# Loading both inputs of a batched matmul through one DMA queue, with the cast moved from the DMA to VectorE

## The chip, the cores and the metric

The kernel runs on one core of a Trainium2 chip. A core has TensorE (PE, matrix products, with its weight loads shown as PEld), VectorE (DVE), ScalarE (ACT), GpSimd (POOL) and SyncE (SP). Data moves between the chip's memory (HBM) and the core's SBUF by 16 DMA engines. Three engines issue transfers: SyncE (its queue is q1 in the profile), ScalarE (q10) and GpSimd (q0; in this kernel some of its transfers also convert fp32 to bf16 on the way). The metric is the device time of one execution in microseconds.

## The reference

```python
def setup_inputs():
    return {
        "a": np.random.randn(1024, 64, 64).astype(np.float32),
        "b": np.random.randn(1024, 64, 64).astype(np.float32),
    }

def reference(a, b):
    return np.matmul(a, b).astype(np.float32)
```

There are 1024 independent products of 64x64 matrices. a and b are read once (16.78 MB each) and the output of 16.78 MB is written once.

## The kernel before

Work is cut into tiles of 64 batches: `n_t` = 16 tiles, t = 0 to 15. a is handled in `n_s` = 8 parts of 128 batches, s = 0 to 7, so part s serves tiles 2s and 2s+1. One part of a is 2 MiB, made of four quarters h of 512 KiB with 4 KB rows (`a_v`); one tile of b is 1 MiB in runs of 512 B (`b_v`); one tile of output is 1 MiB (`o_v`). All operands are turned to bf16 before the products.

What happens to a part of a: `load_a(s)` brings it in. For s = 1 to 7, GpSimd's queue loads three quarters and converts them to bf16 during the transfer (`a_sb`, line 73), and SyncE's queue loads the fourth as fp32 (`a_raw`, line 77). Part 0 is different: `load_first_a` brings all four quarters as fp32, two by SyncE and two by ScalarE, into two tiles of the output pool (line 90). `regroup(s)` then builds `a_bf`, with the four quarters interleaved: for s = 0 four conversions shared by VectorE and ScalarE (line 105), else on VectorE one copy of 3072 bf16 elements per partition (line 108) and one conversion of 1024 (line 111). `transpose(s, j)` turns it on TensorE, pairs of bf16 seen as one fp32 (line 120), and ScalarE copies the result out of PSUM into `at_sb` (line 123).

What happens to a tile t: `spread(t)` makes four VectorE copies into a block-diagonal operand `at_bd` (line 133; two such buffers). `cast(t)` converts the tile of b: on VectorE (line 144), for t = 0 on ScalarE, and for the last tile in four pieces, two on ScalarE and two on VectorE (lines 149 and 151). `multiply(t)` does 64 products of 128x128 by 128x64 (line 189) and copies the results out of PSUM into `o_sb` by eight copies (line 177), on ScalarE, with two of the eight on VectorE where t is odd. `store(t)` sends the tile to HBM (line 166): from GpSimd's queue for t below 14, from SyncE's and ScalarE's for 14 and 15.

`load_b(t)` uses SyncE's queue for even t and ScalarE's for odd t (line 96). `a_pool` and `b_pool` have three buffers for each kind of tile, `o_pool` eight, `work` two. A load waits until the tile that had its buffer before has been used: b(t+3) waits for the cast of b(t).

The order of the work is written out by hand, and each engine carries out its instructions in that order. Before the loop, a part 0, b tiles 0 and 1, a part 1, b tile 2 and a part 2 are loaded, and part 0 is regrouped, transposed and spread. Iteration t then does spread(t+1) and cast(t+1), `load_b(t+3)`, for even t a load of a, transposes, multiply(t), for even t the regroup of part t/2+2, and store(t-1). So, on VectorE, the regroup stands behind the cast of the next tile, and in the last iterations the cast of the last tile stands in front of ScalarE's copies of tile 14. On GpSimd loads of a and stores share one instruction stream; on ScalarE the loads of odd b tiles stand among its copies.

Of the kernel before, what the change touches and what calls it, by code (L numbers as in the profile page):

```python
# [8 lines left out]
fp32 = mybir.dt.float32  # L9
bf16 = mybir.dt.bfloat16  # L10
# [3 lines left out]
def kernel(  # L14
# [14 lines left out]
    nc = tc.nc  # L29
    B, M, K = a.shape  # L30
    _, _, N = b.shape
    assert (M, K, N) == (64, 64, 64) and B % 128 == 0

    n_t, n_s = B // 64, B // 128
    A_AHEAD = 3
# [4 lines left out]
    a_v = a.rearrange("(s g h) (mp v) k -> s h g mp (v k)", h=4, g=32, v=16)  # L40
    b_v = b.rearrange("(t g h) (kp u) n -> t (h kp) g (u n)", h=4, g=16, u=2)
# [3 lines left out]
    a_pool = ctx.enter_context(tc.tile_pool(name="a_pool", bufs=A_AHEAD))  # L45
    b_pool = ctx.enter_context(tc.tile_pool(name="b_pool", bufs=B_AHEAD))
    work = ctx.enter_context(tc.tile_pool(name="work", bufs=2))
    o_pool = ctx.enter_context(tc.tile_pool(name="o_pool", bufs=8))
    t_psum = ctx.enter_context(
        tc.tile_pool(name="t_psum", bufs=4, space=bass.MemoryType.PSUM)  # L50
    )
# [9 lines left out]
    a_tiles, b_tiles, abf_tiles, at_tiles, bbf_tiles = {}, {}, {}, {}, {}  # L61
# [6 lines left out]

    def load_a(s):

        a_sb = a_pool.tile([128, 3, 16, 64], bf16, name="a_sb")
        for h in range(3):
            nc.gpsimd.dma_start(  # L73
                out=a_sb[:, h, :, :].rearrange("p v k -> p (v k)"), in_=a_v[s, h], single_packet=True
            )
        a_raw = a_pool.tile([128, 16, 64], fp32, name="a_raw")
        nc.sync.dma_start(out=a_raw[:].rearrange("p v k -> p (v k)"), in_=a_v[s, 3])  # L77
        a_tiles[s] = a_sb, a_raw

    def load_first_a():  # L80

        raw = [
            o_pool.tile([128, 8, 2, 2, 64], fp32, name="o_sb")[:].rearrange(
                "p gh j wl n -> p (gh j wl n)"
            )
            for _ in range(2)
        ]
        parts = [raw[h % 2][:, 1024 * (h // 2) : 1024 * (h // 2) + 1024] for h in range(4)]
        for h in range(4):
            (nc.scalar if h % 2 else nc.sync).dma_start(out=parts[h], in_=a_v[0, h])  # L90
        a_tiles[0] = parts

    def load_b(t):
        b_sb = b_pool.tile([128, 16, 128], fp32, name="b_sb")
        queue = nc.scalar if t % 2 else nc.sync
        queue.dma_start(out=b_sb[:], in_=b_v[t])  # L96
        b_tiles[t] = b_sb

    def regroup(s):
        a_sb = a_tiles.pop(s)  # L100
        a_bf = work.tile([128, 16, 4, 64], bf16, name="a_bf")
        if s == 0:
            for h in range(4):
                copy = nc.scalar.copy if h % 2 else nc.vector.tensor_copy
                copy(a_bf[:, :, h, :], a_sb[h].rearrange("p (v k) -> p v k", v=16))  # L105
        else:
            cast_sb, raw = a_sb
            nc.vector.tensor_copy(  # L108
                a_bf[:, :, 0:3, :], cast_sb[:].rearrange("p h v k -> p v h k")
            )  # L110
            nc.vector.tensor_copy(a_bf[:, :, 3, :], raw[:])  # L111
        abf_tiles[s] = a_bf
        at_tiles[s] = work.tile([128, 2, 32, 2, 4, 4], fp32, name="at_sb")

    def transpose(s, j):
        a_cols = abf_tiles[s][:].rearrange("p v h k -> p v (h k)").bitcast(fp32)
        for wl in range(2):
            at_ps = t_psum.tile([128, 4, 128], fp32, name="at_ps")
            for vo in range(4):
                nc.tensor.transpose(  # L120
                    at_ps[:, vo, :], a_cols[:, 4 * vo + 2 * j + wl, :], identity[:]
                )
            nc.scalar.copy(  # L123
                at_tiles[s][:, j, :, wl, :, :],
                at_ps[:].rearrange("p vo (g mp) -> p g mp vo", mp=4),
            )

    def spread(t):
        half = slice(16 * (t % 2), 16 * (t % 2) + 16)
        bd = bd_tiles[t % N_BD]  # L130
        for h in range(4):
            rows = slice(32 * h, 32 * h + 32)
            nc.vector.tensor_copy(  # L133
                bd[rows, :, :, :, h, :].rearrange("p j g wl mo -> p j (g wl) mo"),
                at_tiles[t // 2][rows, :, half, :, :, :].rearrange(
                    "p j g wl mp vo -> p j (g wl) (mp vo)"
                ),
            )

    def cast(t):  # L140
        b_bf = work.tile([128, 16, 128], bf16, name="b_bf")
        b_sb = b_tiles.pop(t)
        if t < n_t - 1:
            (nc.vector.tensor_copy if t else nc.scalar.copy)(b_bf[:], b_sb[:])  # L144
        else:
            for gq in range(4):
                rows = slice(4 * gq, 4 * gq + 4)
                if gq % 2:
                    nc.vector.tensor_copy(b_bf[:, rows, :], b_sb[:, rows, :])
                else:  # L150
                    nc.scalar.copy(b_bf[:, rows, :], b_sb[:, rows, :])  # L151
        bbf_tiles[t] = b_bf

    def store(t):
        for piece in held.pop(t):
            piece()
# [51 lines left out]
            held[t] = [lambda q=q: put(q, 8 if whole else 4) for q in ([0] if whole else [0, 4])]  # L208

    with tc.manual_schedule():  # L210
        load_first_a()

        nc.vector.memset(warm[:, 0:1], 0.0)
        nc.scalar.copy(warm[:, 1:2], warm[:, 0:1])  # L214
        load_b(0)
        load_b(1)
        nc.vector.memset(bd_tiles[0][:], 0.0)  # L217
        make_identity(nc, identity)
        nc.gpsimd.memset(bd_tiles[1][:, 0], 0.0)
        load_a(1)  # L220
        load_b(2)
        nc.gpsimd.memset(bd_tiles[1][:, 1], 0.0)
        load_a(2)
        regroup(0)
        transpose(0, 0)
        transpose(0, 1)
        spread(0)
        cast(0)
        for t in range(n_t):
            s, half = t // 2, t % 2  # L230
            if t + 1 < n_t:
                spread(t + 1)
                cast(t + 1)
            if t + B_AHEAD < n_t:
                load_b(t + B_AHEAD)
            if half == 0 and 0 < s < n_s - 1 - A_AHEAD:
                load_a(s + 1 + A_AHEAD)
            if half == 0 and 0 < s < n_s - 1:
                transpose(s + 1, 1)
            multiply(t)  # L240
            if t == 0:
                regroup(1)
                load_a(A_AHEAD)
                load_a(A_AHEAD + 1)
                transpose(1, 0)
                transpose(1, 1)
            elif t == 1:
                regroup(2)
            elif half == 0 and s + 2 < n_s:
                regroup(s + 2)  # L250
            if half == 1 and s + 2 < n_s:
                transpose(s + 2, 0)
            if t >= HOLD - 1:
                store(t - HOLD + 1)
        for t in range(n_t - HOLD + 1, n_t):
            store(t)
# [30 lines left out]
```

## Time and profile before

| | before |
|---|---|
| time, median of 3 runs | 135.07 us (134.95 to 135.22) |
| span of the profiled execution, first to last instruction | 133.4 us (no total of its own is given for this execution) |
| busy: DVE, ACT, PE, PEld, POOL | 94.6, 87.9, 64.4, 61.1, 33.0 us |
| queue q0 (GpSimd): packets, MB, share of the 16 engines | 6832, 20.19, 50.1% |
| queue q1 (SyncE) | 7120, 14.68, 30.4% |
| queue q10 (ScalarE) | 5056, 9.96, 19.7% |
| issue to landing: a by GpSimd, a by SyncE, stores by GpSimd (medians) | 16.4, 18.7, 21.6 us |
| b tiles, issue to landing, shortest, median and longest | 14.8, 16.8, 25.2 us |

How to read it: the span starts with the first instruction of the core. A busy share is an average over all stages. Megabytes of the queues are counted on the written side, so a load that turns fp32 into bf16 counts half of what it reads. A share above 100% for the DMA engines means that packets of several queues overlap on one engine. A row of the timeline gives start and duration in us, engine, line, operation, destination and source, and in square brackets how long the engine was idle before it and what ended that.

### The profile page before, as it was taken

What the parts mean: (1) busy time and instruction counts of PE and PEld (TensorE: products, weight loads), DVE (VectorE), ACT (ScalarE), POOL (GpSimd) and SP (SyncE); (2) the same over time, 40 slices, a digit from 0 to 9 for tenths busy, and PEclk for the clock granted to TensorE, in tenths of its full rate; (3) what the DMA queues carried; (4) which work ended last, traced back from release to release, by engine and by line L of the source; (5) the groups of instructions that cost most, each with busy time, mean ns of one, the idle gap of its engine ahead of it and who ended that gap; (6) DMA issues with size and microseconds to landing.
All of it is one profiled execution on the core that took longest, in us unless ns stands there. A gap on an engine that the chain in (4) does not pass through costs nothing.

```text
span 133.4 us, 2837 instructions
## 1 busy us (share of the span) xinstructions
PE 64.4 (48%) x1152; PEld 61.1 (46%) x1152; DVE 94.6 (71%) x120; ACT 87.9 (66%) x161; POOL 33.0 (25%) x43
## 2 busy tenths in 40 slices
PE   0006406960089384289518970956197363970000
PEld 0006306950089274189418950945196363960000
DVE  5930399109998809995999699959999995987000
ACT  3225424999036998969595969696968969099600
POOL 8991000420090070341233021203020410300000
PEclk9999975797557999856985699599959955599555
DMA  3999999999999999999999999999999999999990
GB/s 77 371 329 311 307 311 281 284 306 325 327 312 401 316 320 333 399 384 397 311 281 375 406 389 351 304 316 390 394 396 387 396 392 391 402 405 398 382 319 18
DMA packets 19021, 45.01 MB, mean 337 GB/s; under 512 B 1088, under 2 KB 3136, under 8 KB 19008
## 3 DMA queue, kind: packets, MB, share of 16 engines
q0 software_dynamic: 6832, 20.19, 50.1%
q1 hardware_dynamic: 7120, 14.68, 30.4%
q10 hardware_dynamic: 5056, 9.96, 19.7%
q8 instruction: 9, 0.15, 0.4%
q14 instruction: 4, 0.03, 0.1%
HBM read 33.55 MB, written 16.78 MB: 377 GB/s over the span
## 4 chain that ended last, share of the span: by engine, by line
DMA 53%; DVE 15%; ACT 13%; PE 6%; issue 5%; SPq 2%; DVEq 0%; ACTq 0%
DMA b_sb<-in_b_dram 53%; ACT o_sb L177 9%; DVE at_bd L133 6%; PE o_ps L189 4%; DVE b_bf L144 4%; DVE o_sb L177 3%; PE at_ps L120 2%; ACT at_sb L123 2%; ACT b_bf L144 1%; SPq L90 1%; DVE a_bf L108 1%; SPq L96 1%; ACT b_bf L151 1%; DVE a_bf L111 0%; SPq L77 0%
## 5 line engine op out<-in xcount | busy, mean ns | idle before, releaser
L177 ACT COPY o_sb<-o_ps 64x512 f32<-64x512 f32 x106 | 61.5, 580 | 10.3 <-PE o_ps L189 9.0
L189 PEld LDWEIGHTS <-at_bd 128*128 128x128 bf16 x1024 | 42.3, 113 | 39.5 <-DVE b_bf L144 25.7
L189 PE MATMUL o_ps<-b_bf,at_bd 128*128 128x64 bf16 x960 | 42.6, 216 | 35.4 <-DVE b_bf L144 23.4
L133 DVE COPY at_bd<-at_sb 32x1024 f32<-32x1024 f32 x64 | 46.9, 733 | 14.1 <-ACT at_sb L123 11.8
L120 PE MATMUL at_ps<-identity,a_bf 128*128 128x128 f32 x128 | 21.2, 335 | 19.4 <-ACT a_bf L105 11.2
L166 POOL DMA_DIRECT2D out_dram<-o_sb x14 | 15.4, 1097 | 56.9 <-ACT at_sb L123 23.4
L120 PEld LDWEIGHTS at_ps<-identity,a_bf 128*128 128x128 f32 x128 | 19.3, 180 | 19.5 <-issue 19.5
L123 ACT COPY at_sb<-at_ps 128x512 f32<-128x512 f32 x32 | 17.5, 590 | 11.0 <-PE at_ps L120 7.8
L144 DVE CAST b_bf<-b_sb 128x2048 bf16<-128x2048 f32 x14 | 17.8, 1271 | 9.6 <-DMA b_sb<-in_b_dram 9.4
L73 POOL DMA_DIRECT2D a_sb<-in_a_dram x21 | 13.6, 662 | 26.4 <-DVE a_bf L108 19.4
L177 DVE COPY o_sb<-o_ps 64x512 f32<-64x512 f32 x14 | 9.7, 690 | 0.3
L108 DVE COPY a_bf<-a_sb 128x3072 bf16<-128x3072 bf16 x7 | 6.7, 950 | 0.0
L105 ACT CAST a_bf<-o_sb 128x1024 bf16<-128x1024 f32 x2 | 2.1, 1044 | 5.2 <-DMA o_sb<-in_a_dram 5.2
L111 DVE CAST a_bf<-a_raw 128x1024 bf16<-128x1024 f32 x7 | 4.8, 683 | 0.0
L144 ACT CAST b_bf<-b_sb 128x2048 bf16<-128x2048 f32 x1 | 1.9, 1900 | 3.9 <-DMA b_sb<-in_b_dram 3.9
L105 DVE CAST a_bf<-o_sb 128x1024 bf16<-128x1024 f32 x2 | 2.8, 1382 | 1.9 <-DMA o_sb<-in_a_dram 1.9
L217 DVE MEMSET at_bd<- 128x4096 f32 x1 | 3.5, 3472 | 0.8 <-issue 0.8
L177 DVE COPY o_sb<-at_ps 64x256 f32<-64x256 f32 x8 | 3.4, 422 | 0.5 <-PE at_ps L189 0.4
L151 ACT CAST b_bf<-b_sb 128x512 bf16<-128x512 f32 x2 | 1.1, 615 | 3.6 <-DMA b_sb<-in_b_dram 3.6
L177 ACT COPY o_sb<-at_ps 64x256 f32<-64x256 f32 x8 | 2.9, 366 | 0.1
L214 ACT ACT_TABLE_LOAD x1 | 1.3, 1283 | 2.3 <-issue 2.3
L189 PE MATMUL at_ps<-b_bf,at_bd 128*128 128x64 bf16 x64 | 2.0, 193 | 1.0 <-DVE at_bd L133 1.0
(12 smaller groups left out, 6.1 us busy)
## 6 DMA issues: line engine op xcount, KB each, us to landing
out_dram<-o_sb POOLq DMA_DIRECT2D x14, 1024.0 KB, 21.6
a_sb<-in_a_dram POOLq DMA_DIRECT2D x21, 256.0 KB, 16.4
a_raw<-in_a_dram SPq DMA_DIRECT2D x7, 512.0 KB, 18.7
o_sb<-in_a_dram SPq DMA_DIRECT2D x2, 512.0 KB, 5.9
o_sb<-in_a_dram ACTq DMA_DIRECT2D x2, 512.0 KB, 7.1
out_dram<-o_sb SPq DMA_DIRECT2D x2, 512.0 KB, 7.5
out_dram<-o_sb SPq DMA_DIRECT2D x2, 256.0 KB, 7.8
out_dram<-o_sb ACTq DMA_DIRECT2D x2, 256.0 KB, 5.5
```

The lines of the kernel that those rows point to most:

```text
L73: nc.gpsimd.dma_start(out=a_sb[:, h, :, :].rearrange("p v k -> p (v k)"), in_=a_v[s, h], single_packet=True)
L105: copy(a_bf[:, :, h, :], a_sb[h].rearrange("p (v k) -> p v k", v=16))
L108: nc.vector.tensor_copy(a_bf[:, :, 0:3, :], cast_sb[:].rearrange("p h v k -> p v h k"))
L111: nc.vector.tensor_copy(a_bf[:, :, 3, :], raw[:])
L120: nc.tensor.transpose(at_ps[:, vo, :], a_cols[:, 4 * vo + 2 * j + wl, :], identity[:])
L123: nc.scalar.copy(at_tiles[s][:, j, :, wl, :, :], at_ps[:].rearrange("p vo (g mp) -> p g mp vo", mp=4),)
L133: nc.vector.tensor_copy(bd[rows, :, :, :, h, :].rearrange("p j g wl mo -> p j (g wl) mo"), at_tiles[t // 2][rows, :, half, :, :, :].rearrange(
L144: (nc.vector.tensor_copy if t else nc.scalar.copy)(b_bf[:], b_sb[:])
L166: store_queue(t, lo).dma_start(out=o_v[t, :, lo : lo + n, :], in_=o_sb[:, lo : lo + n].rearrange("p gh j wl n -> p (gh j wl n)"),)
L177: copies[2 * par + wl](dst, src)
L189: nc.tensor.matmul(o_ps[:, gl, g % 2, j, :], at_bd[:, j, g, :, u], b_bf[:, g, 64 * u : 64 * u + 64], start=(u == 0), stop=(u == 1),)
L217: nc.vector.memset(bd_tiles[0][:], 0.0)
```

## The change

All of a is loaded as fp32 by SyncE's queue (part 0 still half by ScalarE's), into one tile of four quarters, and all of b as well. Loads stand in one stream in the order: part 0 of a, b0, b1, a1, b2, a2, and then in iteration t, for even t, a part t/2+3, followed by b(t+3). The regroup becomes a single VectorE operation that converts 4096 elements per partition from fp32 to bf16 while it interleaves the quarters. GpSimd issues only the stores of tiles 0 to 13, ScalarE only its half of part 0 and its stores of the last tile. Part 0 no longer borrows tiles of `o_pool`, which has seven buffers instead of eight. Products, transposes, spreads, copies out of PSUM and stores stay as they were.

```diff
-    o_pool = ctx.enter_context(tc.tile_pool(name="o_pool", bufs=8))
+    o_pool = ctx.enter_context(tc.tile_pool(name="o_pool", bufs=7))
...
     def load_a(s):
 
-        a_sb = a_pool.tile([128, 3, 16, 64], bf16, name="a_sb")
-        for h in range(3):
-            nc.gpsimd.dma_start(
-                out=a_sb[:, h, :, :].rearrange("p v k -> p (v k)"), in_=a_v[s, h], single_packet=True
-            )
-        a_raw = a_pool.tile([128, 16, 64], fp32, name="a_raw")
-        nc.sync.dma_start(out=a_raw[:].rearrange("p v k -> p (v k)"), in_=a_v[s, 3])
-        a_tiles[s] = a_sb, a_raw
-
-    def load_first_a():
-
-        raw = [
-            o_pool.tile([128, 8, 2, 2, 64], fp32, name="o_sb")[:].rearrange(
-                "p gh j wl n -> p (gh j wl n)"
-            )
-            for _ in range(2)
-        ]
-        parts = [raw[h % 2][:, 1024 * (h // 2) : 1024 * (h // 2) + 1024] for h in range(4)]
+        a_sb = a_pool.tile([128, 4, 16, 64], fp32, name="a_sb")
         for h in range(4):
-            (nc.scalar if h % 2 else nc.sync).dma_start(out=parts[h], in_=a_v[0, h])
-        a_tiles[0] = parts
+            queue = nc.scalar if s == 0 and h % 2 else nc.sync
+            queue.dma_start(out=a_sb[:, h, :, :].rearrange("p v k -> p (v k)"), in_=a_v[s, h])
+        a_tiles[s] = a_sb
 
     def load_b(t):
         b_sb = b_pool.tile([128, 16, 128], fp32, name="b_sb")
-        queue = nc.scalar if t % 2 else nc.sync
-        queue.dma_start(out=b_sb[:], in_=b_v[t])
+        nc.sync.dma_start(out=b_sb[:], in_=b_v[t])
         b_tiles[t] = b_sb
...
             for h in range(4):
                 copy = nc.scalar.copy if h % 2 else nc.vector.tensor_copy
-                copy(a_bf[:, :, h, :], a_sb[h].rearrange("p (v k) -> p v k", v=16))
+                copy(a_bf[:, :, h, :], a_sb[:, h, :, :])
         else:
-            cast_sb, raw = a_sb
-            nc.vector.tensor_copy(
-                a_bf[:, :, 0:3, :], cast_sb[:].rearrange("p h v k -> p v h k")
-            )
-            nc.vector.tensor_copy(a_bf[:, :, 3, :], raw[:])
+            nc.vector.tensor_copy(a_bf[:], a_sb[:].rearrange("p h v k -> p v h k"))
...
-        load_first_a()
+        load_a(0)
...
             if t + 1 < n_t:
                 spread(t + 1)
                 cast(t + 1)
+            if half == 0 and s + A_AHEAD < n_s:
+                load_a(s + A_AHEAD)
             if t + B_AHEAD < n_t:
                 load_b(t + B_AHEAD)
-            if half == 0 and 0 < s < n_s - 1 - A_AHEAD:
-                load_a(s + 1 + A_AHEAD)
             if half == 0 and 0 < s < n_s - 1:
                 transpose(s + 1, 1)
             multiply(t)
             if t == 0:
                 regroup(1)
-                load_a(A_AHEAD)
-                load_a(A_AHEAD + 1)
                 transpose(1, 0)
```

## The prediction

> **What bounds the kernel now.** I read the page from the top: share of engines, the 40 slices, the queues, the chain that ended last, the groups. Then the DMA queues and the engines by stretch, and at the end the timeline of the last 40 us.
>
> From the page of before:
>
> ```profile
> span 133.4 us, 2837 instructions
> DMA  3999999999999999999999999999999999999990
> ...
> HBM read 33.55 MB, written 16.78 MB: 377 GB/s over the span
> ...
> DMA 53%; DVE 15%; ACT 13%; PE 6%; issue 5%; SPq 2%; DVEq 0%; ACTq 0%
> ...
> L144 DVE CAST b_bf<-b_sb 128x2048 bf16<-128x2048 f32 x14 | 17.8, 1271 | 9.6 <-DMA b_sb<-in_b_dram 9.4
> ...
> L108 DVE COPY a_bf<-a_sb 128x3072 bf16<-128x3072 bf16 x7 | 6.7, 950 | 0.0
> ...
> L111 DVE CAST a_bf<-a_raw 128x1024 bf16<-128x1024 f32 x7 | 4.8, 683 | 0.0
> ```
>
> No compute engine is over 71% busy, the DMA slices are full from first to last, and the chain runs 53% through arrivals of b. 50.33 MB cross HBM. The kernel is bound by DMA, so the question is whether bytes move faster, and what is left to do when the last ones land.
>
> The busy time by stretch (us, engines, TensorE clock, DMA share, GB/s as counted on the written side):
>
> ```profile
> 10.00:28.00 18.00, 10.04 (x131) 9.71 (x132) 8.17 (x11) 10.05 (x16) 2.13 (x4) 0.81 1.08 299
> 90.00:116.80 26.80, 16.57 (x332) 15.76 (x333) 24.57 (x32) 19.26 (x36) 5.82 (x5) 0.75 1.03 393
> 116.80:125.00 8.20, 2.42 (x72) 2.17 (x69) 5.41 (x12) 7.91 (x16) 0.09 (x1) 0.92 1.03 398
> ```
>
> The queues (packets, MB, share of 16 engines) from 10 to 20 us, then from 20 to 28 us:
>
> ```profile
> q0 software_dynamic: 518, 0.93, 49.3%
> q1 hardware_dynamic: 518, 1.19, 33.5%
> q10 hardware_dynamic: 494, 0.98, 25.4%
> ```
>
> ```profile
> q0 software_dynamic: 501, 0.92, 60.5%
> q1 hardware_dynamic: 504, 1.10, 39.4%
> q10 hardware_dynamic: 133, 0.27, 8.6%
> ```
>
> q0 is GpSimd's queue, q1 SyncE's, q10 ScalarE's. No store is out yet before 28 us, so q0 carries only casting loads, which read two bytes for each byte written. In bytes read, 10 to 28 us is 2x(0.93+0.92)+1.19+1.10+0.98+0.27 = 7.24 MB in 18 us: 402 GB/s. Without casts, with stores, it is 393 to 398. So the ceiling is nearly the same for all mixes: about 400 GB/s. The second thing to see is that queues with work send equal numbers of packets (518, 518, 494).
>
> The timeline at the end, DVE then ACT:
>
> ```profile
> 94.88 1.24 DVE b_bf L144
> ```
>
> ```profile
> 96.02 0.95 DVE L108 COPY a_bf<-a_sb 128x3072 bf16<-128x3072 bf16 x1
> 96.89 0.69 DVE L111 CAST a_bf<-a_raw 128x1024 bf16<-128x1024 f32 x1
> ...
> 112.33 1.23 DVE L144 CAST b_bf<-b_sb 128x2048 bf16<-128x2048 f32 x1 [1.47 <-DMA b_sb<-in_b_dram]
> ```
>
> ```profile
> 116.88 1.14 ACT L151 CAST b_bf<-b_sb 128x512 bf16<-128x512 f32 x2 [3.59 <-DMA b_sb<-in_b_dram]
> 118.04 4.73 ACT L177 COPY o_sb<-o_ps 64x512 f32<-64x512 f32 x8
> ...
> 125.85 0.38 ACTq L166 DMA_DIRECT2D out_dram<-o_sb  x1
> ```
>
> (The first line, from the chain, is the cast of b tile 11.) All loads have landed at 116.84. The DMA engines then still carry 398 GB/s x 8.2 us = 3.26 MB and, from 125 on, 1.80 MB: 5.06 MB of stores, which cover the last computation. That overlap is what before does well: loads ran ahead of stores, since two or three of the busy queues were load queues. Stores waited.
>
> **The change part by part.** I sum against the profiled span of 133.4 us. The page gives no total time for that execution; the median of the runs is 135.07, so 1.7 us lie around the span, and I add them at the end.
>
> *Bytes.* HBM bytes don't change: 21 casting loads become fp32 loads of the same 11.0 MB read. Whether a non-casting load is faster isn't shown directly. Nearest rows: 402 GB/s with half of the bytes cast, 393 where only b and stores move, and 422 to 430 in the two microseconds (5 to 7 us) in which mostly a's first fp32 rows move. I take 402 for loads, the row with no stores in it, and 395 for stores, between 393 and 398. Ends: 393 and 426.
>
> The Trainium skill, DMA: Bandwidth & Descriptors, section SWDGE vs HWDGE vs iDMA, gives 408.7 GB/s for one load stream from SP with 4 KiB rows. By it the loads below would take 1.2 us less and the sum would be 135.7; a has 4 KB rows, b has 512 B runs, and no row here shows SyncE's queue alone for long.
>
> *Issue.* ScalarE loses 8 issues of b (0.69 us each, 5.6 us), GpSimd 21 (13.6 us busy). SyncE gets 46 loads in place of 17; at 0.53 to 0.73 us each that is some 30 us of 133 on an engine that does nothing else. The order of instructions with their waits shows that each of its loads waits for the load eight before it; eight loads are 4 to 8 MB, over 10 us of transfer at 402, so the queue doesn't run dry. a(s+3) also waits for the regroup of s, two iterations of s earlier; b(t+3) for the cast of t. Queued behind such a wait on SyncE are only loads needed later. Cost zero, hidden by the loads already out; were that cover gone, it is rival C. o_pool 8 to 7 costs nothing: the two tiles that held a's first rows are gone, and a store has seven tiles' time, some 50 us, where it took 21.6 to land.
>
> *Start.* a0 still comes by SyncE and ScalarE, then b0, b1, a1 in order. Before, b0 landed at 19.26 us because a1, a2 and b1 shared the engines. After, a0 and b0 are 3.15 MB: 2.4 + 3.15/0.402 = 10.2 us. The products of tile 0 start some 6 us earlier (transposes and copies of a's first part took until 15.4, and a0 now lands some 2.5 us sooner). It gains nothing by itself, because the engines were full anyway; but stores start earlier too and now take engine time from loads.
>
> *Regroup.* 950 + 683 = 1633 ns become one cast of 4096 elements. Not shown; by rows: the 2048-element cast takes 1226 and the 1024-element one 683, so 543 per further 1024 and 683 + 3x543 = 2312 ns. Ends: 1633 (no cost) and 4x683 = 2732. I take 2312: +0.68 us, seven times 4.7 us. Six lie beside the wait for loads (one s moves 4 MB of loads and 2 MB of stores, 16 us; DVE needs 8 spreads at 0.73, 2 casts, 2 copies at 0.69 and the regroup, 12.1 us). The seventh, after b11, is on the path: +0.68.
>
> *Where the path now ends.* The last a part (a7) goes out just before b11, and from the cast of tile 11 on the rest is a fixed run of DVE work. When does b11 land? Ahead of it are 28 MiB of loads (16 of a, 12 of b), 29.36 MB: 73.0 us. Stores by then: only one store queue and one load queue are left, so by equal packets a store gets at least half the engines (4 KB packets against a's 4 KB; b's are 2 KB) and lands in some 5 us, while tiles come every 8: stores keep up. Of tiles 0 to 10, 10.4 MiB or 10.9 MB have gone: 27.6 us. First bytes move at 2.4 us. So b11 lands at 2.4+73.0+27.6 = 103.0. In before its cast began at 94.88.
>
> The page's rule in Rules for kernel authors is that spreading DMAs over queues does not help bandwidth; by that rule alone the number of queues is no matter and the time stays 135.1. The same page, section Queues, rings and completion order, has the engines take queues in turn by packet, as the 518, 518 and 494 show: the total rate stays, the division between loads and stores doesn't.
>
> From the cast of b11 to that of b14, before took 112.33-94.88 = 17.45 us, 1.47 of it waiting for b14. After, b14 and b15 are early enough (all loads and 12.3 MiB of stores are through at 2.4+83.5+32.7 = 118.6): 17.45-1.47+0.68 = 16.7, so 119.7. ScalarE's copies of tile 14 can start when half its matmuls are done, about 3.1 us later (before: 113.6 to 117.2 for both halves): 122.8. From their start to the last store's issue before took 125.85-118.04 = 7.8: 130.6. That store landed 5.4 us later behind the backlog. Without one: at most 5.4, at least the 0.7 us that its 256 KB take at 395 GB/s; I take 3.2, the middle. Before, the span ended 1.0 to 1.9 us after the last landing; 1.4. End 135.2, and with 1.7 around it **136.9 us**: +8.1 at b11, +0.7 regroup, -1.5 wait for b14, -5.5 backlog and late b15.
>
> **The rivals.**
> - B, faster. Loads on SyncE's queue, fp32 without cast, run like the 422 to 430 row. At 426 the 29.36 MB take 68.9 us, b11 lands at 98.9, the end is 132.8. It decides from 413 GB/s on (1.85 us saved). For it: the 5 to 7 us rows. Against: half the load bytes are b, and b with stores gives 393.
> - C, a lone load queue can't fill the engines. Nearest row: 116.8 to 125 us, where one queue moved 2.90 MB, 354 GB/s (another had 11.5% of the time). About half the loads travel with no store beside them; 14.7 MB at 354 cost 4.9 us: 141.8. Against: three full queues were no faster than this one and a bit.
> - D, DVE becomes the bound (94.6+4.7 us busy): if all seven regroups count, +4.0 on the sum, 140.9. Against: 12.1 of 16 us per s.
> - E, no difference: loads keep their share, the last lands near 116.8, stores pile up behind it as before, 135.1. For it: the engines are full either way.
>
> **How the numbers follow.** A (forecast) 0.50, B 0.20, C 0.13, D 0.07, E 0.10. A's own range: loads at 411 to 391 GB/s move it by -1.6 to +2.1 and the landing by -2.5 to +2.2; half of each end together gives 134.9 to 139.0. The whole range reaches to B (132.8) and D (141.0); beyond lie C's upper part and rates over 426, some 0.17. A measurement of this kernel tells 0.2% (0.27 us) from no change. Faster is B, 0.20; same is E, 0.10; slower A, C and D, 0.70.
>
> **What would show it.** No q10 loads behind a's first part and q0 only stores; ScalarE's cast of b0 near 13 us instead of 19.3; regroups of 2.3 us; the cast of b11 waiting for DMA and starting near 103; full DMA slices until about 120 and then thinning, instead of full to the end; under 4.2 MB moved after the last load. A cast of b11 under 101 means B; DMA slices below 9 or under 380 GB/s before 100 us mean C; casts late with their b long landed mean D; 5 MB of stores after the last load mean E.

## The result and the profile after

The changed kernel takes 147.05 us (median of 4 runs, 146.57 to 147.82) against 135.01 us for the kernel before in the same session: a ratio of 1.0898, 95% interval 1.0859 to 1.0936. The profiled execution, the longest of the four, took 147.82 us with a span of 146.1 us, so 1.7 us lie around the span, as in the kernel before.

From the page of the kernel after, in the order of the lines shown of before:

```profile
span 146.1 us, 2824 instructions
DMA  4999999999999999999999999999999999995992
GB/s 91 399 330 291 381 366 335 406 413 419 311 363 333 388 380 365 352 365 418 360 351 353 412 406 318 385 356 411 393 326 369 390 315 290 315 400 214 332 339 92
HBM read 33.55 MB, written 16.78 MB: 345 GB/s over the span
DMA 34%; SPq 25%; DVE 24%; issue 4%; PE 4%; ACT 3%; DVEq 0%
L123 DVE CAST b_bf<-b_sb 128x2048 bf16<-128x2048 f32 x14 | 17.2, 1227 | 25.1 <-DMA b_sb<-in_b_dram 24.9
L90 DVE CAST a_bf<-a_sb 128x4096 bf16<-128x4096 f32 x7 | 16.0, 2288 | 0.0
out_dram<-o_sb POOLq DMA_DIRECT2D x14, 1024.0 KB, 9.9
```

The row of busy tenths is as full as before. The row below it isn't: until the last loads are in, the rate swings between 290 and 419 GB/s. The DMA engines are busy, but for long stretches they are busy slowly. VectorE now waits 24.9 us for b instead of 9.4. The regroup takes 2288 ns. Stores land 9.9 us after their issue instead of 21.6.

Busy time of the kernel after in three stretches (us, then PE, PEld, DVE, ACT, POOL, TensorE clock, DMA share, GB/s):

```profile
10.00:15.00 5.00, 3.46 (x16) 3.24 (x16) 0.56 (x1) 3.17 (x6) 0.00 (x0) 1.00 1.05 290
25.00:30.00 5.00, 4.18 (x76) 4.03 (x74) 1.96 (x3) 3.90 (x7) 0.33 (x1) 0.79 1.03 406
120.00:127.00 7.00, 3.40 (x97) 3.19 (x94) 6.77 (x10) 5.10 (x9) 2.71 (x2) 0.94 1.06 292
```

And what the queues of the kernel after did from 120 to 126 us (packets, MB, share of 16 engines):

```profile
DMA packets 874, 1.75 MB, mean 291 GB/s; under 512 B 24, under 2 KB 24, under 8 KB 873
q1 hardware_dynamic: 873, 1.74, 105.1%
```

Only SyncE's queue is at work there, in packets of 2 KB: these are tiles of b, whose rows are runs of 512 B. At 105% share they move 291 GB/s. (One queue alone shows this share, so a share above 100% doesn't need packets of several queues, as the reading guide has it.) From 25 to 30 us mostly a's 4 KB rows and a store move 406. Counting microsecond by microsecond in the queue view, b is by itself (GpSimd's queue sends under ten packets, and the packets of the load queues average 1.5 to 3 KB, so most are b's) in 38 microseconds of the kernel after, and in none of the kernel before.

### The profile page after: what moved, and what is told of

Read it like the earlier page. It is cut to its first block, busy times and chain, and to the rows that moved or that the text cites. A ratio compares the mean times of both kernels' runs of the same rounds, so it can differ in the third digit from the quotient of the medians.

```text
span 146.1 us, 2824 instructions
## 1 busy us (share of the span) xinstructions
PE 66.7 (46%) x1152; PEld 63.3 (43%) x1152; DVE 97.0 (66%) x113; ACT 88.3 (60%) x153; POOL 22.6 (15%) x22
## 2 busy tenths in 40 slices
DMA packets 19020, 50.51 MB, mean 346 GB/s; under 512 B 1088, under 2 KB 3136, under 8 KB 19008
## 4 chain that ended last, share of the span: by engine, by line
DMA 34%; SPq 25%; DVE 24%; issue 4%; PE 4%; ACT 3%; DVEq 0%
DMA b_sb<-in_b_dram 30%; SPq L74 15%; DVE at_bd L112 11%; SPq L79 10%; DVE a_bf L90 6%; DVE o_sb L156 5%; DMA a_sb<-in_a_dram 4%; PE at_ps L99 2%; DVE b_bf L123 2%; ACT o_sb L156 2%; PE o_ps L168 1%; PE at_ps L168 1%; ACT at_sb L102 0%; DVEq L259 0%; DVEq L112 0%
## 5 line engine op out<-in xcount | busy, mean ns | idle before, releaser
L168 PEld LDWEIGHTS <-at_bd 128*128 128x128 bf16 x1024 | 43.1, 114 | 53.0 <-DVE b_bf L123 44.8
L168 PE MATMUL o_ps<-b_bf,at_bd 128*128 128x64 bf16 x960 | 43.5, 218 | 48.5 <-DVE b_bf L123 42.4
L112 DVE COPY at_bd<-at_sb 32x1024 f32<-32x1024 f32 x64 | 46.3, 724 | 11.4 <-ACT at_sb L102 9.7
L145 POOL DMA_DIRECT2D out_dram<-o_sb x14 | 18.4, 1314 | 110.2 <-ACT o_sb L156 43.9
L123 DVE CAST b_bf<-b_sb 128x2048 bf16<-128x2048 f32 x14 | 17.2, 1227 | 25.1 <-DMA b_sb<-in_b_dram 24.9
L99 PE MATMUL at_ps<-identity,a_bf 128*128 128x128 f32 x128 | 22.4, 349 | 20.2 <-ACT a_bf L88 10.3
L99 PEld LDWEIGHTS at_ps<-identity,a_bf 128*128 128x128 f32 x128 | 20.6, 189 | 20.3 <-issue 20.3
L90 DVE CAST a_bf<-a_sb 128x4096 bf16<-128x4096 f32 x7 | 16.0, 2288 | 0.0
L88 ACT CAST a_bf<-a_sb 128x1024 bf16<-128x1024 f32 x2 | 2.1, 1044 | 4.4 <-DMA a_sb<-in_a_dram 4.4
L88 DVE CAST a_bf<-a_sb 128x1024 bf16<-128x1024 f32 x2 | 1.3, 662 | 2.7 <-DMA a_sb<-in_a_dram 2.7
L198 POOL MEMSET at_bd<- 128x2048 f32 x1 | 1.8, 1799 | 0.0
L201 POOL MEMSET at_bd<- 128x2048 f32 x1 | 1.8, 1799 | 0.0
```

The costliest lines, as they stand in the source:

```text
L88: copy(a_bf[:, :, h, :], a_sb[:, h, :, :])
L90: nc.vector.tensor_copy(a_bf[:], a_sb[:].rearrange("p h v k -> p v h k"))
L99: nc.tensor.transpose(at_ps[:, vo, :], a_cols[:, 4 * vo + 2 * j + wl, :], identity[:])
L112: nc.vector.tensor_copy(bd[rows, :, :, :, h, :].rearrange("p j g wl mo -> p j (g wl) mo"), at_tiles[t // 2][rows, :, half, :, :, :].rearrange(
L145: store_queue(t, lo).dma_start(out=o_v[t, :, lo : lo + n, :], in_=o_sb[:, lo : lo + n].rearrange("p gh j wl n -> p (gh j wl n)"),)
L168: nc.tensor.matmul(o_ps[:, gl, g % 2, j, :], at_bd[:, j, g, :, u], b_bf[:, g, 64 * u : 64 * u + 64], start=(u == 0), stop=(u == 1),)
```

## The experiments

The first theory after the result, S: b's short runs, when they have a queue to themselves, keep the engines slow. Rivals: D, the loads only lose engine time to the stores (the forecast's own mechanism); Q, one queue can't fill the engines; O, b waits behind a in one stream; R, VectorE's longer regroup.

### What each kind of transfer reaches by itself

The first probe computes nothing; it moves 8 MiB per phase and waits for all of it before the next phase.

> Loads alone, six phases of 8 MiB each, no computation (the output is only partly written, with zeros). b tiles in 512 B runs through SyncE's queue; the same through SyncE's and ScalarE's in turn; a in 4 KB rows through SyncE's; the same bytes of b as contiguous 8 KB rows through SyncE's; b through SyncE's beside a through ScalarE's; b through SyncE's beside stores by GpSimd. Theory S (short runs of b in a single queue keep the engines slow, 290 GB/s from 10 to 15 us of the changed kernel): phase 1 near 290 GB/s, phase 2 near 380 to 400, phases 3 and 4 near 400 to 415, phases 5 and 6 near 380 to 400. Theory D (the loads only lose engine time to stores): all phases near 400. Theory Q (one queue can't fill the engines, whatever its rows): phases 1, 3 and 4 alike and below phase 2.

The stores had nothing to wait for, so they went out in the first phase instead of the last. In the rows below, stretch by stretch: b beside stores; b on two queues; a on SyncE's queue; b as contiguous 8 KB rows; b beside a; b alone on SyncE's queue.

```profile
10.00:40.00 30.00, 0.00 (x0) 0.00 (x0) 0.47 (x1) 1.00 1.03 397
55.00:78.00 23.00, 0.00 (x0) 0.32 (x1) 0.00 (x0) 1.00 1.06 290
90.00:102.00 12.00, 0.00 (x0) 0.00 (x0) 0.00 (x0) 1.00 1.03 415
108.00:125.00 17.00, 0.00 (x0) 0.00 (x0) 0.00 (x0) 1.00 1.01 426
135.00:144.00 9.00, 0.00 (x0) 0.00 (x0) 0.00 (x0) 1.00 1.04 358
156.00:184.00 28.00, 0.00 (x0) 0.00 (x0) 0.00 (x0) 1.00 1.04 289
```

Q falls: one queue reaches 415 and 426 GB/s. S as stated falls too: two queues of b are no faster than one, 290 and 289. What is slow is b's transfer itself. Beside a it stays slow (358 for the pair: a packet of a at 415 GB/s takes 158 ns of an engine, one of b at 290 takes 113 ns, and 6 KB in 271 ns on 16 engines is 363, so the two simply add). Beside stores it is hidden: 397. That is theory S2: b's cost is hidden by stores, and not by loads of a.

A second probe completed the table.

> Transfers alone, in phases, no computation (the output is only partly written, with zeros): b through SyncE's queue; the same beside 4 stores; a in 4 KB rows beside 4 stores; a with the cast through GpSimd's queue; casting loads beside b; 8 stores alone. The first probe showed b at 290 GB/s through one queue and through two, a at 412, b beside a at about 350, b beside stores at about 395. Theory S2 (b's 512 B runs occupy an engine's reading for 116 ns per 2 KB packet, whatever the queue; stores run beside that, other loads don't): b beside stores 390 to 400 while both run; a beside stores 405 to 425; casts alone about 410 of bytes read; casts beside b additive, about 350 of bytes read. If casting loads are cheaper than fp32 loads (the reading of 10 to 28 us of before at 402 GB/s): casts alone above 430 of bytes read, beside b above 380. Stores alone 395 to 430.

b alone; b beside stores; a beside stores; casting loads of a alone (counted on the written side); casting loads, with b beside them; stores alone. The columns are VectorE, GpSimd, clock, DMA share, GB/s:

```profile
10.00:28.00 18.00, 0.00 (x0) 0.00 (x0) 1.00 1.06 290
38.00:46.00 8.00, 0.00 (x0) 0.00 (x0) 1.00 1.03 402
90.00:104.00 14.00, 0.00 (x0) 0.00 (x0) 1.00 1.02 414
111.00:126.00 15.00, 0.00 (x0) 4.63 (x9) 1.00 1.12 205
131.00:146.00 15.00, 0.00 (x0) 3.05 (x6) 1.00 1.07 266
160.00:184.00 24.00, 0.00 (x0) 3.44 (x4) 1.00 0.97 320
```

Casting loads alone read 2 x 205 = 410 GB/s, no cheaper than the same rows without the cast (415). Stores alone move 320, less than the 395 to 430 that was expected. S2 had expected casting loads and b simply to add, some 350 in bytes read; but beside b they help. The queues from 139 to 146 us:

```profile
q0 software_dynamic: 491, 0.91, 68.5%
q1 hardware_dynamic: 489, 0.97, 40.3%
```

In bytes read that is (2 x 0.91 + 0.97) MB in 7 us, 398 GB/s, where fp32 rows of a beside b gave 358. One after the other, at 410 and 290, the same bytes would take 7.8 us, so part of b's cost is hidden, not all. So in the kernel before two things hid b: stores, and the loads that cast. The change removed the second, and the first turned out to be shorter.

### Long rows in the kernel after

```diff
-    b_v = b.rearrange("(t g h) (kp u) n -> t (h kp) g (u n)", h=4, g=16, u=2)
+    b_v = b.rearrange("(t x) (y z) n -> t (x y) (z n)", x=64, y=2)
...
-        nc.sync.dma_start(out=b_sb[:], in_=b_v[t])
+        nc.sync.dma_start(out=b_sb[:].rearrange("p g c -> p (g c)"), in_=b_v[t])
```

> The changed kernel, but each b tile is read as contiguous 8 KB rows, so b's elements stand in the wrong places and the products are not the reference's; bytes, queues, order and work are the same. Theory S: b no longer slows its queue, so the forecast's sum holds: 135 to 139 us. Theory D (division between loads and stores) and theory R (VectorE's longer regroup, seven times 0.65 us): nothing of these is touched, so it stays within 1.5 us of 147. Theory Q: stays near 147.

134.61 us, ratio to before 0.9991 (0.9974 to 1.0009), just below what S expected. Nothing but the rows of b changed, and 12.4 us went. Its page:

```profile
span 133.1 us, 2808 instructions
GB/s 71 409 433 416 409 431 398 410 394 426 428 409 414 419 414 411 405 414 424 415 414 414 408 432 424 406 416 406 433 417 425 414 421 408 367 75 230 333 341 48
L90 DVE CAST a_bf<-a_sb 128x4096 bf16<-128x4096 f32 x7 | 16.0, 2288 | 0.0
```

The dips to 290 are gone. D, O and R are all still in this kernel (stores land after 11.8 us, one stream, the same regroup), so none of them by itself is the 12 us. Rows of 8 KB also come in larger packets (12,876 in all instead of 19,020) and read HBM in another order of addresses, so length of run, size of packet and order of addresses are not told apart here, nor in the probes.

### b on other queues of the kernel after

```diff
-        nc.sync.dma_start(out=b_sb[:], in_=b_v[t])
+        queue = nc.scalar if t % 2 else nc.sync
+        queue.dma_start(out=b_sb[:], in_=b_v[t])
```

> The changed kernel, with odd b tiles on ScalarE's queue again. Theory S: b's packets are taken in turn with a's or with another b's, so they overlap and the loss goes: 133 to 138 us. Theory D: three queues again, two of them loads: back near 136 to 138 by the other division. Theory O (in a single queue a's 2 MiB stand in front of the b tile that is needed next): likewise better, since odd b tiles pass a; the probe and the kernel with long rows tell S from O. Theory R: 145 to 147.

150.25 us, ratio 1.1145 (1.1123 to 1.1167): worse than the change, where S, D and O had expected better and R no change. This is what refuted S in its first form, together with the probe. From 10 to 15 us two queues of b send 356 and 354 packets and move 295 GB/s. O falls here as well: VectorE now waits 11.0 us for a, so letting odd b tiles pass a makes a late.

All of b on ScalarE's queue (`nc.scalar.dma_start` in the same place):

> The changed kernel, with all b on ScalarE's queue and a on SyncE's. Theory S2: b and a run side by side, which doesn't hide b's cost; 143 to 149. Theory O (b waits behind a in one queue): b is no longer behind a: 136 to 141. Theory D (share of the loads against the stores): two load queues of three: 136 to 141.

149.45 us, ratio 1.1107 (1.1071 to 1.1143), as S2 had it: side by side with a, b is still not hidden. How much of the 2 to 3 us above the change is order and how much ScalarE's waits was not tried.

### One part of the change at a time

Only b's queue, in the kernel before:

```diff
-        queue = nc.scalar if t % 2 else nc.sync
-        queue.dma_start(out=b_sb[:], in_=b_v[t])
+        nc.sync.dma_start(out=b_sb[:], in_=b_v[t])
```

> The kernel before, with all b on SyncE's queue and nothing else changed. Theory S: while a's casting loads run (to about 90 us) b overlaps with them and with stores; afterwards b is alone only where no store is out: 136 to 141 us. Theory D: stores get ahead of the loads, as forecast for the change: 136 to 138. Theory R: 135.1, no regroup is touched.

140.38 us, ratio 1.0411 (1.0393 to 1.0429): +5.6, within S's range and above D's. Stores now land after 10.3 us:

```profile
out_dram<-o_sb POOLq DMA_DIRECT2D x14, 1024.0 KB, 10.3
```

With one load queue less, stores get through in half the time, are gone sooner, and leave b by itself: by the count used above, for 14 microseconds (38 in the kernel after, none in the kernel before).

Only the cast, in the kernel before:

```diff
-    o_pool = ctx.enter_context(tc.tile_pool(name="o_pool", bufs=8))
+    o_pool = ctx.enter_context(tc.tile_pool(name="o_pool", bufs=7))
...
-        a_sb = a_pool.tile([128, 3, 16, 64], bf16, name="a_sb")
+        a_sb = a_pool.tile([128, 3, 16, 64], fp32, name="a_sb")
```

> The kernel before, with GpSimd's three quarters of a loaded as fp32 on the same queue (VectorE's copy of 3072 elements then converts too), seven output tiles instead of eight, b on two queues as before. The probes showed b beside casting loads at about 398 GB/s of bytes read and b beside fp32 rows of a at 350. Theory S2: the casts covered part of b, so b beside a costs more now; 11.0 MB of a went beside some 5.5 MB of b: 16.5 MB at 350 instead of 398 is +5.7 us, less where stores take over the cover: 137 to 141. If the cast matters only through VectorE's work (7 x 0.5 us, hidden): 135.

142.07 us, ratio 1.0531 (1.0516 to 1.0546): +7.1, at the upper end of what S2 gave. Stores still land after 23.0 us and b is by itself in no microsecond; what is gone is the cover by the casts. The two parts, +5.6 and +7.1, add up to 12.7, close to the 12.0 of the whole change.

### Long rows in the kernel before, with and without the cast

The same edit of b's rows in the kernel before (e4 below) and in the one without the cast (e9; e7 is that kernel with short runs):

> The kernel before, with each b tile read as contiguous 8 KB rows (b's elements stand in the wrong places, so the products are not the reference's). Theory S2 with cover: in the kernel before b nearly always has stores or casts beside it, so long rows gain little: 132.5 to 135. Without cover (b is as slow in the kernel before, and the casts are what made up for it): 125 to 130.

> The kernel of e7 (a loaded as fp32 everywhere, b on two queues) with each b tile read as contiguous 8 KB rows (products are not the reference's). Theory S2: without the short runs the casts have nothing to cover, so taking them away costs little: 132 to 135.5 against 142.1 of e7 and 132.0 of e4. If casting loads are worth their time by themselves (half the written bytes), it stays 5 us or more above e4: 137 to 139.

131.98 us (0.9793, 0.9761 to 0.9826) and 131.97 us (0.9781, 0.9759 to 0.9803); both just under the ranges that S2 gave. Without short runs the cast in the DMA is worth nothing; with them it is worth 7 us. VectorE's added conversion of 0.80 us per part (1753 instead of 957 ns in these two runs) and the output tile less cost nothing in this kernel. So the cost of b's short runs is the difference in each row:

| kernel | b in 512 B runs | b in 8 KB rows | cost of the runs |
|---|---|---|---|
| before | 134.7 | 132.0 | 2.7 |
| before, a without cast | 142.1 | 132.0 | 10.1 |
| after | 147.05 | 134.6 | 12.4 |

(The rows mix sessions; the kernel before took 134.7 to 135.0 us in all of them.) The rest of the change, read down the long-row column, is +2.6 us; no run splits it further.

### Making stores last longer

```diff
-            return nc.gpsimd
+            return nc.scalar
```

> The changed kernel, with the stores of tiles 0 to 13 on ScalarE's queue, where stores had 1 KB packets in the kernel before. Theory S2: stores then get one packet of 1 KB for each of 2 or 4 KB of the loads, last longer and cover more of b: 138 to 144. Theory O: 146 to 149, the loads' order is the same. If 14 issues of about 1 us on ScalarE matter more than cover: above 147.

140.54 us, ratio to before 1.0429 (1.0399 to 1.0459), 6.5 us less than the change. Stores of 1 KB packets take their turn against 2 and 4 KB packets of the loads and land after 15.6 us instead of 9.9:

```profile
DMA packets 29773, 50.52 MB, mean 364 GB/s; under 512 B 1088, under 2 KB 17472, under 8 KB 29760
out_dram<-o_sb ACTq DMA_DIRECT2D x14, 1024.0 KB, 15.6
```

The same bytes, loads in the same order; the stores lie beside b for longer, and b is by itself (no stores, counted as above) in 18 microseconds instead of 38. This recovers about half. The stores' queue and packet size changed together here.

### Two candidates

Casting all four quarters of a in the kernel before (the fourth leaves SyncE's queue, and the regroup is one bf16 copy):

> The kernel before, with all four quarters of parts 1 to 7 of a cast on GpSimd's queue and regrouped by one bf16 copy; SyncE's queue has no a. Theory S2: a fourth more packets that cover b, and VectorE saves about 0.5 us a part: 132.5 to 135. If the seven more issues on GpSimd and the longer queue in front of the stores weigh more: 135 to 137.

134.8 us, ratio 0.9991 (0.9977 to 1.0006): no difference. With that, all b on SyncE's queue and the stores on ScalarE's:

> A candidate: all quarters of parts 1 to 7 of a cast on GpSimd's queue, all b on SyncE's, stores of tiles 0 to 13 on ScalarE's queue in 1 KB packets. Theory S2: b has casts and slow stores beside it nearly always: 132 to 136. If one packet of 1 KB in turn lets stores pile up until ScalarE waits for output tiles, or the 14 issues hold up its copies: above 137.

136.76 to 139.34 us, median 138.61, ratio 1.0235 (1.0162 to 1.0307): slower, by an amount that the spread leaves open; why was not followed up. No run that computes the reference's products beat the kernel before.

## Why the prediction was wrong

It gave 136.9 (132.8 to 141.0); the direction was right, the size wrong by 10 us. Step by step along its own chain, in us of the span:

| step | forecast | measured |
|---|---|---|
| cast of tile 11 of b starts | 103.0 | 110.24 |
| from there to the cast of tile 14 | 16.7 | 18.0 |
| to ScalarE's first copy of tile 14 | 3.1 | 3.2 |
| to the last store's issue | 7.8 | 7.8 |
| landing and end | 4.6 | 6.8 |
| end of the span | 135.2 | 146.1 |

The measured rows come from the timelines of VectorE and ScalarE in the kernel after:

```profile
110.24 1.23 DVE L123 CAST b_bf<-b_sb 128x2048 bf16<-128x2048 f32 x1 [3.30 <-DMA b_sb<-in_b_dram]
118.19 1.23 DVE L123 CAST b_bf<-b_sb 128x2048 bf16<-128x2048 f32 x1 [1.78 <-DMA b_sb<-in_b_dram]
128.25 1.23 DVE L123 CAST b_bf<-b_sb 128x2048 bf16<-128x2048 f32 x1
```

```profile
131.46 4.74 ACT L156 COPY o_sb<-o_ps 64x512 f32<-64x512 f32 x8 [0.17 <-PE o_ps L168]
139.28 0.44 ACTq L145 DMA_DIRECT2D out_dram<-o_sb  x1
```

The step that failed is "the ceiling is nearly the same for all mixes: about 400 GB/s" and with it "I take 402 for loads", the term of 73.0 us for the loads ahead of tile 11. The 402 was read from a stretch in which b ran beside casting loads, and the 393 from one in which it ran beside stores: both rows had b under cover, and I used them for a kernel in which b moves by itself for 38 microseconds, at 305 GB/s on average. At 402 the bytes of that time would take some 9 us less (an estimate from these two rates). No microsecond of before shows b alone, and the lower bound (393) came from a covered row. So the cast of tile 11 starts 7.2 us later than forecast, and the wait for tile 12 (1.78 us), which the sum had at zero, comes on top.

With b in long rows, in the otherwise same kernel, the cast of tile 11 (the one ahead of the last regroup) starts at 98.19:

```profile
98.19 1.23 DVE L123 CAST b_bf<-b_sb 128x2048 bf16<-128x2048 f32 x1 [3.36 <-DMA b_sb<-in_b_dram]
99.33 2.29 DVE L90 CAST a_bf<-a_sb 128x4096 bf16<-128x4096 f32 x1
104.39 1.23 DVE L123 CAST b_bf<-b_sb 128x2048 bf16<-128x2048 f32 x1
```

The rows of b move this cast by 12.05 us, nearly the whole 12.4 us of the time. And 98.19 is not the forecast's 103.0 but near rival B's 98.9: without the cost of the short runs the loads run faster than 402, with it slower. That this kernel took 134.61 us, not far from the forecast's 136.9, is thus no sign that the sum was right in its parts.

- *Division between loads and stores:* right in direction. Stores land in 9.9 us instead of 21.6 (the forecast had some 5), and the kernel with only b's queue changed shows the same. The price was named wrongly: what hurts is not mainly that loads get a smaller share (all that is left with long rows is 2.6 us), but that the stores run out and no longer hide b. That the direction of the time came out is in part luck: with long rows the changed kernel is as fast as the kernel before (0.9991), so the forecast's own mechanism doesn't make the 12 us.
- *The cast costs nothing to lose, since HBM bytes don't change:* wrong by 7.1 us, though only because of b's runs.
- *Regroup 2312 ns:* measured 2288. That it is hidden but for the last was not tested by itself in this kernel.
- *Issue on SyncE hidden:* the engines stayed full, so the cover held, but the price was wrong. The sum had 0.53 to 0.73 us for each issue; the issues of b take 3.1 us in the median and up to 11.3, and SyncE's queue is 25% of the chain that ended last (2% before). With long rows the same issues take 0.33 us and that share is 1%, so the long issues come with the short runs; whether they only follow from the slow transfers was not tested.
- *Landing 3.2 us without a backlog:* too short (and the middle of 0.7 and 5.4 is 3.05). Stores by themselves move at 320 GB/s in the probe, and the last ones landed in 5.7 to 5.9 us (medians), with no loads beside them.
- *The start:* ScalarE's cast of the first b tile began at 14.31 instead of 19.29; forecast near 13.
- *Rival C* came nearest, 141.8, by a wrong mechanism: a lone queue fills the engines well with a's rows (415). Its case had the right symptom, slow loads with no store beside them. *Rival B* fell: a's rows alone do reach 415, b's don't; its rate came with the long rows. *Rival D* fell: VectorE was busy 97.0 us and waited for b. *Rival E* fell: full slices, but a lower rate.

## What to carry to other kernels

A full row of DMA busy tenths doesn't mean that bytes move at the ceiling; read the GB/s row beside it, and read a transfer's rate where it is alone. A rate taken from a mix holds only for that mix: before moving a transfer to another queue or another time, ask what hid its cost and whether that is still beside it afterwards. Here a cast in the DMA and slow stores looked like waste and were the cover of b's short runs.

## What was not expected of the hardware

- Loads of b in 512 B runs (2 KB packets) move 290 GB/s on one queue or on two, the same bytes as contiguous 8 KB rows 426. The Trainium skill, DMA: Bandwidth & Descriptors, section Specifications, names 512 B as the smallest transfer at line rate; this load, with nothing beside it, stays well below the rate of longer rows, though run length was not told apart from packet size and order of addresses.
- Stores hide that cost (397 to 402 GB/s for the pair), casting loads hide much of it (398 in bytes read), fp32 loads with 4 KB rows don't (358). Why is open.
- Spreading b over two queues didn't raise its rate (290 and 289), as the same page's Rules for kernel authors say of spreading in general; but the number of load queues decided how long the stores stayed, and that was worth 5.6 us.
- Stores with nothing beside them reach 320 GB/s, a beside stores 414.
